# Seven block products of 256 columns in place of eight, for eleven channel pairs in two of four feed-forward passes

## The chip, the cores and the metric

The kernel runs on one core of a Trainium2 chip. The metric is the device time of one execution in microseconds. A core has TensorE (PE in the profile), VectorE (DVE), ScalarE (ACT), GpSimd (POOL) and SyncE (SP), which issues the DMAs. Each engine works through its own list of instructions in order and waits at semaphores for the others.

## What is computed

A trunk of two residual layers over 1024 tokens of width 1024, in float32. Layer 0 mixes tokens by gated and by sparse attention, layer 1 by a convolution module; each is followed by the same kind of feed-forward block, which is what the change touches:

```
def conv_ffn(x, w_up, conv_w, conv_b, w_down):
    h = causal_dwconv(x @ w_up, conv_w, conv_b)      # 1024 -> 5632 channels, 3 taps along the sequence
    g, u = jnp.split(h, 2, axis=-1)
    return (jax.nn.gelu(g) * u) @ w_down             # 2816 -> 1024
...
    for layer in range(DEPTH):
...
        x = layer_norm(ALPHA * x + mix, ln_mix_g[layer], ln_mix_b[layer])
        ffn = conv_ffn(x, ffn_w_up[layer], ffn_conv_w[layer], ffn_conv_b[layer], ffn_w_down[layer])
        x = layer_norm(ALPHA * x + ffn, ln_ffn_g[layer], ln_ffn_b[layer])
```

## The kernel before

The 1024 tokens are worked on in two halves of 512, so there are four feed-forward passes: `F00` (half 0, layer 0), `F10` (half 1, layer 0), `F01` (half 0, layer 1) and `F11` (half 1, layer 1). Every float32 product is made of three matmuls: each operand is split into a high part, rounded to the type fp32r, and a low remainder, and `mm3` (L76 to L79) adds high by low, low by high and high by high. `split` (L61) makes the high part on ACT and the low part by a subtraction on DVE or POOL; `wload` (L65) loads a block of weights of 128x1024 and splits it, the high part `wh` on ACT (L70), the low part `wl` in two halves on POOL (L73). There are three buffers each for the raw block `wraw`, for `wh` and for `wl`.

A pass has 22 channel pairs, a gate channel tile and a value channel tile of 128 channels each. `up(j)` computes the two tiles of pair j: eight blocks of the input width, 24 matmuls of 512 columns for each tile, into a PSUM bank `pu`. Then come the three convolution taps: ACT writes the first from PSUM to `acc` (L677), DVE adds the other two (L681, L682), and in half 0 the last two tokens are copied to `halo` (L684) for half 1, which computes its corrections `cor` from them at its start (L661 to L666). ACT takes the gelu of the gate tile (L687), POOL multiplies the two tiles (L689) and makes the low part `pl` of the product (L63), ACT its high part `ph`. The down product runs in three groups of 8, 8 and 6 pairs; a unit of it is 24 matmuls of 512 columns with one weight block, into the banks `pd`, which DVE adds to the residual `Z` (L396, L398). In the last pass the third group keeps its weights on chip and ends with the final layer norm, token tile by token tile (`down_last`).

A layer norm (`normed`, L623 and L624) works on `Z` with two vectors `gb`, of which there are two buffers; `norm` transposes the result on PE (`pn`, L635) and splits it into the next operand `XT`. The main program interleaves generators: each `yield` hands over to another chain. The order of the instructions on each engine is then set by a scheduler, within what the data and the buffers allow, so that it isn't the written one.

Of the kernel before, what the change touches and what calls it, by code (L numbers as in the profile page):

```python
# [10 lines left out]
F32 = mybir.dt.float32  # L11
F32R = mybir.dt.float32r
# [9 lines left out]
EPS = 1e-5  # L22
NPAIR = 22
KG = [(0, 8), (8, 16), (16, 22)]
FW = 1152
F2W = 256

# [10 lines left out]
def trunk_kernel(ctx, tc, xt, wab, wv, w280, wst, sgub, sgulg, sgulb, pe_k, pe_v, w1k, w1v, w2k, w2v,  # L38
# [10 lines left out]
    def A(tag, dtype=F32, shape=(128, 8, 512), name="A"):  # L49
        return ap.tile(list(shape), dtype, name=name, tag=tag, bufs=2)  # L50
# [25 lines left out]
    def mm3(out_, ah, al, bh, bl, first, last):  # L76
        nc.tensor.matmul(out_, ah, bl, start=first, stop=False)  # L77
        nc.tensor.matmul(out_, al, bh, start=False, stop=False)  # L78
        nc.tensor.matmul(out_, ah, bh, start=False, stop=last)  # L79

    def mtile(out_, w, xh, xl, kn=8):
        wh, wl = w
# [69 lines left out]
    def col(n, i):  # L152
        return V[n][:, i:i + 1]
# [448 lines left out]
    def tmp(name, w=512, bufs=4):  # L602
        return fp.tile([128, w], F32, name=name, tag="t", bufs=bufs)
# [47 lines left out]
    hal = fp.tile([128, 44, 2], F32, name="halo")  # L651
    cor = fp.tile([128, 44, 2], F32, name="cor")

    def ffn(h, l, tail=None):
        xh, xl = XT[h]
        z = Z[h]
        cw = V[f"fw{l}"].rearrange("p (m k) -> p m k", k=3)
# [8 lines left out]
                nc.vector.tensor_tensor(cor[:, :, i], cor[:, :, i], V[cb], op=OP.add)  # L666
        prod = {}

        def up(j):
            acc = []  # L670
            for e in range(2):
                mt = 2 * j + e
                w = wload(wup[l, mt])
                p = psn("u", "pu")
                mtile(p, w, xh, xl)
                a = tmp("acc")
                nc.scalar.activation(a[:, 2 * h:], p[:, 2 * h:], AF.Identity, scale=cw[:, mt, 2:3], bias=col(cb, mt))  # L677
                for i in range(2 * h):
                    nc.scalar.activation(a[:, i:i + 1], p[:, i:i + 1], AF.Identity, scale=cw[:, mt, 2:3],  # L679
                                         bias=cor[:, mt, i:i + 1])  # L680
                nc.vector.scalar_tensor_tensor(a[:, 1:], p[:, :511], cw[:, mt, 1:2], a[:, 1:], op0=OP.mult, op1=OP.add)  # L681
                nc.vector.scalar_tensor_tensor(a[:, 2:], p[:, :510], cw[:, mt, 0:1], a[:, 2:], op0=OP.mult, op1=OP.add)  # L682
                if h == 0:
                    nc.vector.tensor_copy(hal[:, mt, :], p[:, 510:512])  # L684
                acc.append(a)
                if e == 0:
                    nc.scalar.activation(a, a, AF.Gelu_apprx_tanh)  # L687
                    yield
            nc.gpsimd.tensor_tensor(acc[0], acc[0], acc[1], op=OP.mult)  # L689
            hi = fp.tile([128, 512], F32R, name="ph", tag="p", bufs=18)  # L690
            lo = fp.tile([128, 512], F32R, name="pl", tag="p", bufs=18)
            split(hi, lo, acc[0], nc.gpsimd)
            prod[j] = (hi, lo)
            yield

        def down_last(tail):
# [22 lines left out]
        def down(gi):  # L719
            j0, j1 = KG[gi]  # L720
            return product(lambda k: prod[j0 + k], lambda dh, b: wdn[l, gi * 8 + dh * 4 + b], j1 - j0,
                           into(h, gi == 0, gi == 2))

        done = 0
        for gi, (j0, j1) in enumerate(KG):
            top = min(j1 + 1, NPAIR)
# [255 lines left out]
```

## Time and profile before

| | |
|---|---|
| time, median of 3 runs | 2336.21 us (2334.55 to 2337.54) |
| the profiled execution | 2339.19 us |
| its span, first to last instruction | 2337.4 us |
| busy share of the span | PE 98%, DVE 50%, ACT 43%, POOL 59% |
| mean granted TensorE clock | 0.993 |

The first row is what the prediction is measured against. The durations of instructions come from one profiled execution, which is a little longer than the median. Its busy shares are means over stages that differ; what a stage is limited by is read from a stretch of it. Matmuls are pipelined: the time one of them takes in a row is longer than the distance between the starts of two of them, and it is the distance that counts.

### The profile page before, as it was taken

The page shows a single profiled execution, that of the slowest core. Times are in us where ns is not written, and L with a number is a line of the kernel's source. Part 1 is how long each engine was busy: PE and PEld are TensorE (multiplying, and loading weights), DVE is VectorE, ACT ScalarE, POOL GpSimd, SP SyncE. Part 2 cuts the span into 40 slices and gives each one's busy share as a digit, 9 for nine tenths or more (in the row PEclk, how much of TensorE's full clock was granted, in tenths as well). Part 3 has the DMA queues.
Part 4 walks back from the last instruction along what each step waited for, and adds up shares of the span by engine and source line. Part 5 has one row for each costly group of instructions (what it writes and reads, how often), then busy time and mean ns, then how long its engine had stood idle before and what let it go on. Part 6 is the DMA issues. An engine that isn't in the chain of part 4 may idle for free.

```text
span 2337.4 us, 30072 instructions
## 1 busy us (share of the span) xinstructions
PE 2295.2 (98%) x10959; PEld 1916.0 (82%) x10959; DVE 1174.3 (50%) x2144; ACT 1008.4 (43%) x1786; POOL 1390.4 (59%) x1313
## 2 busy tenths in 40 slices
PE   9999899999999999999999999999999999999998
PEld 7889789887888888788888887788888887888886
DVE  3532889656322223579972326589961446212214
ACT  4133998733433323433343552433242633534441
POOL 4442776566665656655566576655566666666672
PEclk9999999999999999999999999999999999999999
DMA  6053121353223323222323233232332233323340
GB/s 230 31 145 96 51 64 53 116 185 104 90 95 99 98 92 99 81 97 93 99 93 97 90 109 109 81 96 94 99 97 93 90 108 135 97 94 98 99 135 36
DMA packets 82987, 232.22 MB, mean 99 GB/s; under 512 B 10079, under 2 KB 24039, under 8 KB 82840
## 3 DMA queue, kind: packets, MB, share of 16 engines
q1 hardware_dynamic: 82840, 230.30, 31.0%
q8 instruction: 87, 1.43, 0.2%
q14 instruction: 60, 0.49, 0.1%
HBM read 213.44 MB, written 8.43 MB: 95 GB/s over the span
## 4 chain that ended last, share of the span: by engine, by line
PE 92%; DVE 3%; ACT 2%; issue 1%; POOL 1%; DMA 1%; DVEq 0%; ACTq 0%; SPq 0%; POOLq 0%
PE pu L77 14%; PE pu L79 13%; PE pu L78 13%; PE pd L77 9%; PE pd L78 9%; PE pd L79 9%; PE pt L562 2%; PE pcg L78 1%; PE pca L78 1%; PE pcg L77 1%; PE pca L77 1%; PE pca L79 1%; PE pcg L79 1%; DVE P L498 1%; PE O L570 1%
## 5 line engine op out<-in xcount | busy, mean ns | idle before, releaser
L73 POOL TENSOR_TENSOR wl<-wraw,wh 128x512 fp32r<-128x512 f32 x680 | 888.8, 1329 | 706.3 <-ACT wh L70 706.0
L77 PE MATMUL pu<-XTl,wh 128*128 128x512 f32 x1440 | 565.8, 393 | 5.5 <-DVE acc L682 3.7
L79 PE MATMUL pu<-XTh,wh 128*128 128x512 f32 x1440 | 564.2, 392 | 0.0
L78 PE MATMUL pu<-XTh,wl 128*128 128x512 f32 x1440 | 563.7, 391 | 0.0
L70 ACT ACTIVATE wh<-wraw 128x1024 fp32r<-128x1024 f32 x340 | 359.5, 1058 | 413.8 <-PE pd L79 349.1
L681 DVE SCALAR_TENSOR_TENSOR acc<-pu,vec,acc 128x511 f32<-128x511 f32 x176 | 131.7, 748 | 515.1 <-ACT acc L679 267.2
L77 PEld LDWEIGHTS pu<-XTl,wh 128*128 128x128 f32 x1440 | 272.5, 189 | 62.6 <-issue 4.1
L757 DVE SCALAR_TENSOR_TENSOR cacc<-ht,vec,cacc 128x512 f32<-128x512 f32 x464 | 318.5, 750 | 5.5 <-ACT cacc L753 3.9
L677 ACT ACTIVATE acc<-pu,vec 128x510 f32<-128x510 f32 (+1 forms) x176 | 137.1, 779 | 424.3 <-PE pu L79 424.1
L79 PEld LDWEIGHTS pu<-XTh,wh 128*128 128x128 f32 x1440 | 272.1, 189 | 56.7
L78 PEld LDWEIGHTS pu<-XTh,wl 128*128 128x128 f32 x1440 | 272.3, 189 | 56.3
L77 PE MATMUL pd<-wl,ph 128*128 128x512 f32 x656 | 259.2, 396 | 0.0
L78 PE MATMUL pd<-wh,pl 128*128 128x512 f32 x656 | 258.8, 395 | 0.0
L79 PE MATMUL pd<-wh,ph 128*128 128x512 f32 x656 | 256.8, 395 | 0.0
L79 PEld LDWEIGHTS pd<-wh,ph 128*128 128x128 f32 x656 | 123.6, 188 | 28.8
L78 PEld LDWEIGHTS pd<-wh,pl 128*128 128x128 f32 x656 | 123.7, 189 | 28.7
L77 PEld LDWEIGHTS pd<-wl,ph 128*128 128x128 f32 x656 | 123.6, 188 | 28.5
L398 DVE TENSOR_TENSOR Z<-Z,pd 128x512 f32<-128x512 f32 x64 | 43.5, 682 | 180.1 <-PE pd L79 180.0
L682 DVE SCALAR_TENSOR_TENSOR acc<-pu,vec,acc 128x510 f32<-128x510 f32 x176 | 131.5, 747 | 4.7
L689 POOL TENSOR_TENSOR acc<-acc 128x512 f32<-128x512 f32 x88 | 113.6, 1291 | 25.1 <-DVE acc L682 17.6
L396 DVE SCALAR_TENSOR_TENSOR Z<-Z,pd 128x512 f32<-128x512 f32 x64 | 43.6, 681 | 158.3 <-PE pd L79 158.3
L63 POOL TENSOR_TENSOR pl<-acc,ph 128x512 fp32r<-128x512 f32 x88 | 113.7, 1292 | 8.9 <-ACT ph L62 7.4
(251 smaller groups left out, 3778.1 us busy)
## 6 DMA issues: line engine op xcount, KB each, us to landing
wraw<-wup SPq DMA_DIRECT2D x176, 512.0 KB, 3.5
wraw<-wdn SPq DMA_DIRECT2D x82, 512.0 KB, 3.5
wraw<-cwin SPq DMA_DIRECT2D x32, 512.0 KB, 3.5
wraw<-wout SPq DMA_DIRECT2D x16, 512.0 KB, 4.0
wraw<-cwout SPq DMA_DIRECT2D x16, 512.0 KB, 3.5
wraw<-wab SPq DMA_DIRECT2D x14, 512.0 KB, 3.8
gb<-lns SPq DMA_DIRECT2D x12, 512.0 KB, 4.3
B<-fd SPq DMA_DIRECT2D x8, 512.0 KB, 3.8
```

The lines of the kernel that those rows point to most:

```text
L63: (leng or nc.vector).tensor_tensor(lo, src, hi.bitcast(F32), op=OP.subtract)
L70: nc.scalar.activation(wh[:, :n], raw[:, :n], AF.Copy)
L73: (leng or nc.gpsimd).tensor_tensor(wl[:, c], raw[:, c], wh[:, c].bitcast(F32), op=OP.subtract)
L77: nc.tensor.matmul(out_, ah, bl, start=first, stop=False)
L78: nc.tensor.matmul(out_, al, bh, start=False, stop=False)
L79: nc.tensor.matmul(out_, ah, bh, start=False, stop=last)
L562: nc.tensor.transpose(pt[:, j, e * 128:(e + 1) * 128], P[:, e, o:o + kn], ident)
L677: nc.scalar.activation(a[:, 2 * h:], p[:, 2 * h:], AF.Identity, scale=cw[:, mt, 2:3], bias=col(cb, mt))
L681: nc.vector.scalar_tensor_tensor(a[:, 1:], p[:, :511], cw[:, mt, 1:2], a[:, 1:], op0=OP.mult, op1=OP.add)
L682: nc.vector.scalar_tensor_tensor(a[:, 2:], p[:, :510], cw[:, mt, 0:1], a[:, 2:], op0=OP.mult, op1=OP.add)
L689: nc.gpsimd.tensor_tensor(acc[0], acc[0], acc[1], op=OP.mult)
L757: nc.vector.scalar_tensor_tensor(c[0] if k else ht[:, :H], ht[:, k:k + H], dww[:, j, k:k + 1], c[0], op0=OP.mult, op1=OP.add)
```

## The change

In `F00` and `F11` the pairs 5 to 15 are computed by `up7(j)`. It takes the two channel tiles of a pair, the two halves of the input width and the two halves of the 512 tokens as a 2 by 2 by 2 block product, and forms it from seven block products (Winograd's form of Strassen's method) where the plain form has eight. Each is four input blocks by three matmuls of 256 columns, so there are 84 such matmuls for a pair where there were 48 of 512 columns. The seven need sums of blocks of both operands. The sums of the weights are made per pair in `prep(j)`, by four additions on DVE (`ws` and in place in `wraw`), of which three results are split on ACT (`sh`) and DVE (`sl`); the raw blocks `ra` and `rb` themselves are split on ACT and POOL as before. The sums of the input (`TA`, `TB`) are made once per pass in `sums()`, on DVE, POOL and ACT, in the buffers that held the norm vectors, which are therefore loaded a second time for half 0's layer 0. The results are put together from the banks `pa` and `pb` and a copy `tt` by five additions of 256 columns on DVE. In all 22 pairs of these two passes the product of the two tiles and its split are on DVE instead of POOL (`gated`). The down product of these passes comes in units of 24 matmuls, one behind the fifth product of each pair, in groups of four pairs; each pass has 16 more additions to `Z` by that. The code that normalises half 1 is moved behind pair 15 of `F00`, that of the final norm of half 0 behind pair 5 of `F11`.

```diff
+QUICK = (5, 16)
...
-    def ffn(h, l, tail=None):
+    def ffn(h, l, tail=None, quick=False):
...
+        def gated(j, acc):
+            eng = nc.vector if quick else nc.gpsimd
+            eng.tensor_tensor(acc[0], acc[0], acc[1], op=OP.mult)
+            hi = fp.tile([128, 512], F32R, name="ph", tag="p", bufs=18)
+            lo = fp.tile([128, 512], F32R, name="pl", tag="p", bufs=18)
+            split(hi, lo, acc[0], eng)
...
+        def sums():
...
+            for k in (0, 2):
+                u1, u2 = (fp.tile([128, 2, 2, 256], F32, name="ts", tag="nrm", bufs=2) for _ in range(2))
+                b11, b12, b22, b21 = u1[:, 0], u1[:, 1], u2[:, 0], u2[:, 1]
+                nc.gpsimd.tensor_tensor(b11, *f(k, 0), op=OP.add)
+                nc.vector.tensor_tensor(b12, *f(k, 256), op=OP.add)
+                nc.gpsimd.tensor_tensor(b21, *f(k + 4, 0), op=OP.add)
+                nc.vector.tensor_tensor(b22, *f(k + 4, 256), op=OP.add)
+                nc.vector.tensor_tensor(b22, b22, b12, op=OP.subtract)
+                nc.vector.tensor_tensor(b12, b12, b11, op=OP.subtract)
+                nc.vector.tensor_tensor(b11, b22, b11, op=OP.add)
+                nc.vector.tensor_tensor(b21, b21, b11, op=OP.subtract)
+                yield
+                for n, t_, e in (("t2", b11, nc.vector), ("t1", b12, nc.vector), ("t3", b22, nc.gpsimd),
+                                 ("t4", b21, nc.vector)):
+                    split(X7[n][0][:, k:k + 2], X7[n][1][:, k:k + 2], t_, e)
+                yield
+
+        def prep(j):
+            ra, rb = W4(F32, name="wraw"), W4(F32, name="wraw")
+            nc.sync.dma_start(ra, wup[l, 2 * j])
+            nc.sync.dma_start(rb, wup[l, 2 * j + 1])
+            s1, s2 = (fp.tile([128, 512], F32, name="ws", tag="ht", bufs=8) for _ in range(2))
+            a, b = slice(0, 512), slice(512, 1024)
+            add = lambda o, x_, y_, op: nc.vector.tensor_tensor(o, x_, y_, op=op)
...
+            def pair(src):
+                h_, l_ = W4(F32R, name="wh", tag="wh"), W4(F32R, name="wl", tag="wl")
+                nc.scalar.activation(h_, src, AF.Copy)
+                for c in (a, b):
+                    nc.gpsimd.tensor_tensor(l_[:, c], src[:, c], h_[:, c].bitcast(F32), op=OP.subtract)
+                return [(h_[:, c], l_[:, c]) for c in (a, b)]
...
+            add(s1, rb[:, a], rb[:, b], OP.add)
+            add(s2, s1, ra[:, a], OP.subtract)
+            w["11"], w["12"] = pair(ra)
+            w["s2"] = one(s2, nc.vector)
+            w["s1"] = one(s1, nc.vector)
+            yield w
+            add(rb[:, a], ra[:, a], rb[:, a], OP.subtract)
+            add(ra[:, b], ra[:, b], s2, OP.subtract)
+            w["s3"], w["22"] = pair(rb)
+            w["s4"] = one(ra[:, b], nc.vector)
+            yield
...
+        def up7(j):
+            w = W7.pop(j)
+            pa, pb = psn("u", "pa"), psn("c", "pb")
+            t_ = tmp("tt")
+            t_, v_ = t_[:, :256], t_[:, 256:]
+            c0, c1 = slice(0, 256), slice(256, 512)
+            add = lambda o, a, b: nc.vector.tensor_tensor(o, a, b, op=OP.add)
+            prod7(pa[:, c0], w["11"], X7["11"])
+            prod7(pb[:, c1], w["s2"], X7["t2"])
+            nc.scalar.activation(t_, pa[:, c0], AF.Copy)
+            add(t_, t_, pb[:, c1])
+            prod7(pa[:, c0], w["12"], X7["21"], False)
+            nxt = prep(j + 1) if j + 1 < QUICK[1] else None
+            prod7(pa[:, c1], w["s1"], X7["t1"])
+            add(v_, t_, pa[:, c1])
+            if nxt:
+                W7[j + 1] = next(nxt)
+            prod7(pb[:, c0], w["s3"], X7["t3"])
+            add(pb[:, c1], v_, pb[:, c0])
+            yield
+            prod7(pa[:, c1], w["s4"], X7["22"], False)
+            add(pa[:, c1], t_, pa[:, c1])
+            acc = [taps3(2 * j, pa)]
+            nc.scalar.activation(acc[0], acc[0], AF.Gelu_apprx_tanh)
+            prod7(pb[:, c0], w["22"], X7["t4"], False)
+            if nxt:
+                next(nxt)
+            add(pb[:, c0], t_, pb[:, c0])
+            acc.append(taps3(2 * j + 1, pb))
+            gated(j, acc)
+            yield
...
-    F00 = ffn(0, 0)
-    mix(norm(1, g0), F00, 1)
-    go(F00, 56)
+    F00 = ffn(0, 0, quick=True)
+    go(F00, 2 * QUICK[1])
+    g0 = affine(0)
+    mix(norm(1, g0), F00, 2)
+    go(F00, 4)
...
+    F11 = ffn(1, 1, lambda tt: final(1, g3)(tt), quick=True)
+    go(F01)
+    go(F11, 2 * QUICK[0] + 2)
     g3 = affine(3)
-    F11 = ffn(1, 1, final(1, g3))
-    go(F01)
     for tt in range(4):
         final(0, g3)(tt)
-        go(F11, 2)
+        go(F11, 4)
     go(F11)
```

The order on PE in the middle of `F00` before, in the up product of a pair: one bank, three matmuls of 512 columns per input block.

```order
L79 MATMUL pu<-XTh,wh 128x512
L77 MATMUL pu<-XTl,wh 128x512
L78 MATMUL pu<-XTh,wl 128x512
L79 MATMUL pu<-XTh,wh 128x512
L77 MATMUL pu<-XTl,wh 128x512
L78 MATMUL pu<-XTh,wl 128x512
```

The order on PE in the same pass of the change, in the middle of a pair. `pa<-XTh,wl` and its like are the next pair's first product, `pb<-TB,wh` is the seventh product of the pair, on the columns of `pb` that the third of the sums (s3) was multiplied into.

```order
L81 MATMUL pa<-XTh,wh 128x256
L79 MATMUL pa<-XTl,wh 128x256
L80 MATMUL pa<-XTh,wl 128x256
L81 MATMUL pa<-XTh,wh 128x256
L79 MATMUL pb<-TB,wh 128x256
L80 MATMUL pb<-TB,wl 128x256
L81 MATMUL pb<-TB,wh 128x256
```

The products are half as wide, and products of two pairs stand between each other: the first product of the next pair runs ahead of the seventh of this one.

The order on DVE in `F00` before, for one pair: two taps and a halo copy for each tile.

```order
L681 SCALAR_TENSOR_TENSOR acc<-pu,vec,acc 128x511
L682 SCALAR_TENSOR_TENSOR acc<-pu,vec,acc 128x510
L684 COPY halo<-pu 128x2
L681 SCALAR_TENSOR_TENSOR acc<-pu,vec,acc 128x511
L682 SCALAR_TENSOR_TENSOR acc<-pu,vec,acc 128x510
L684 COPY halo<-pu 128x2
```

The order on DVE in `F00` of the change, the second half of a pair's period without `Z` additions: L64 is the low part of a sum of weights (`sl`) or of the product (`pl`), L685 the product, L724 a sum of weights, L771 an addition of 256 columns.

```order
L680 COPY halo<-pb 128x2
L64 TENSOR_TENSOR sl<-ws,sh 128x512
L685 TENSOR_TENSOR acc<-acc 128x512
L64 TENSOR_TENSOR pl<-acc,ph 128x512
L771 TENSOR_TENSOR tt<-tt,pa 128x256
L64 TENSOR_TENSOR sl<-ws,sh 128x512
L724 TENSOR_TENSOR wraw<-wraw,ws 128x512
L771 TENSOR_TENSOR pb<-tt,pb 128x256
L64 TENSOR_TENSOR sl<-wraw,sh 128x512
L771 TENSOR_TENSOR pa<-tt,pa 128x256
L677 SCALAR_TENSOR_TENSOR acc<-pa,vec,acc 128x511
L771 TENSOR_TENSOR pb<-tt,pb 128x256
```

The taps (now L677 and L678) have between them the weight work for the pair after next and the product and its split, which stood on POOL.

The order on POOL in `F00` before, over two pairs with no down unit between them.

```order
L73 TENSOR_TENSOR wl<-wraw,wh 128x512 x2
L689 TENSOR_TENSOR acc<-acc 128x512
L73 TENSOR_TENSOR wl<-wraw,wh 128x512 x2
L63 TENSOR_TENSOR pl<-acc,ph 128x512
L73 TENSOR_TENSOR wl<-wraw,wh 128x512 x2
L689 TENSOR_TENSOR acc<-acc 128x512
L73 TENSOR_TENSOR wl<-wraw,wh 128x512 x2
L63 TENSOR_TENSOR pl<-acc,ph 128x512
```

The order on POOL in `F00` of the change, from pair to pair: the four of L731 are two for `rb` and two for the next `ra`, L74 is the block of down weights.

```order
L731 TENSOR_TENSOR wl<-wraw,wh 128x512 x4
L74 TENSOR_TENSOR wl<-wraw,wh 128x512 x2
L731 TENSOR_TENSOR wl<-wraw,wh 128x512 x4
L74 TENSOR_TENSOR wl<-wraw,wh 128x512 x2
L731 TENSOR_TENSOR wl<-wraw,wh 128x512 x4
L74 TENSOR_TENSOR wl<-wraw,wh 128x512 x2
```

POOL keeps the splits of the unsummed weights alone, in a fixed order of ra, down, rb.

## Rows read from the trace of the kernel before

**Rows 1.** The head of the page: busy time by engine, the chain by engine.

```profile
PE 2295.2 (98%) x10959; PEld 1916.0 (82%) x10959; DVE 1174.3 (50%) x2144; ACT 1008.4 (43%) x1786; POOL 1390.4 (59%) x1313
...
PE 92%; DVE 3%; ACT 2%; issue 1%; POOL 1%; DMA 1%; DVEq 0%; ACTq 0%; SPq 0%; POOLq 0%
```

**Rows 2.** Busy time by window: up products and down products of half 0's pass.

```profile
core 0: us, PE busy (x) PEld busy (x) DVE busy (x) ACT busy (x) POOL busy (x), PEclk, DMA share, GB/s
604.90:659.30 54.40, 54.40 (x242) 45.05 (x241) 15.65 (x31) 23.02 (x31) 37.86 (x30) 1.00 0.31 97
668.90:713.40 44.50, 44.50 (x193) 36.09 (x192) 6.37 (x10) 9.66 (x10) 23.08 (x19) 1.00 0.31 97
```

**Rows 3.** Timeline of PE, 256 columns (start, duration), first and last of 11.

```profile
84.00 0.28 PE L78 MATMUL pg<-wsh,vl 128*128 128x256 f32 x1
...
85.18 0.28 PE L79 MATMUL pg<-wsh,vh 128*128 128x256 f32 x1
```

**Rows 4.** DVE: two neighbours on the timeline, and a group of 256 columns (mean).

```profile
492.39 0.69 DVE L63 TENSOR_TENSOR mt<-mraw,mt 128x512 fp32r<-128x512 f32 x1
493.00 0.69 DVE L400 BATCH_NORM_STATS2 st<-Z 128x6 f32<-128x512 f32 x1
...
L63 DVE TENSOR_TENSOR ptl<-pt,pth 128x256 fp32r<-128x256 f32 x24 | 9.9, 414 | 0.3
```

**Rows 5.** Timelines of ACT, DVE and POOL in one up product.

```profile
641.81 0.78 ACT L677 ACTIVATE acc<-pu,vec 128x512 f32<-128x512 f32 x1 [3.71 <-PE pu L79]
642.48 1.05 ACT L70 ACTIVATE wh<-wraw 128x1024 fp32r<-128x1024 f32 x1
643.43 0.62 ACT L62 ACTIVATE ph<-acc 128x512 fp32r<-128x512 f32 x1
...
643.47 0.75 DVE L682 SCALAR_TENSOR_TENSOR acc<-pu,vec,acc 128x510 f32<-128x510 f32 x1
644.14 0.15 DVE L684 COPY halo<-pu 128x2 f32<-128x2 f32 x1
...
643.61 2.54 POOL L73 TENSOR_TENSOR wl<-wraw,wh 128x512 fp32r<-128x512 f32 x2 [1.65 <-ACT wh L70]
```

**Rows 6.** DMA issues: size of each, microseconds from issue to landing.

```profile
wraw<-wup SPq DMA_DIRECT2D x176, 512.0 KB, 3.5
```

**Rows 7.** Timeline of DVE, correction step of `F10`, POOL quiet.

```profile
905.33 0.19 DVE L663 TENSOR_TENSOR cor<-cor,cor 128x44 f32<-128x44 f32 x1
```

**Rows 8.** Timelines of DVE and POOL, the same step in `F11`.

```profile
1884.83 1.33 DVE L664 TENSOR_TENSOR cor<-halo,vec 128x44 f32<-128x44 f32 x1
1886.08 1.32 DVE L663 TENSOR_TENSOR cor<-cor,cor 128x44 f32<-128x44 f32 x1
...
1884.79 1.30 POOL L63 TENSOR_TENSOR Sl<-nrm,Sh 128x512 fp32r<-128x512 f32 x1
1886.05 1.29 POOL L689 TENSOR_TENSOR acc<-acc 128x512 f32<-128x512 f32 x1
```

**Rows 9.** Timelines of DVE and POOL, final norm at half 1's last pass.

```profile
1959.14 1.28 DVE L623 SCALAR_TENSOR_TENSOR Z<-Z,mv,gb 128x1024 f32<-128x1024 f32 x1
...
1970.06 2.11 DVE L623 SCALAR_TENSOR_TENSOR Z<-Z,mv,gb 128x1024 f32<-128x1024 f32 x1
...
1969.80 3.49 POOL L73 TENSOR_TENSOR wl<-wraw,wh 128x512 fp32r<-128x512 f32 x2
```

**Rows 10.** Timeline of PE at the starts of `F00` and `F11`.

```profile
577.25 1.71 PE L635 MATMUL pn<-ident,Z 128*128 128x128 f32 x8 [2.73 <-DVE XTl L63]
578.66 0.77 PE L77 MATMUL pu<-XTl,wh 128*128 128x512 f32 x1
...
585.41 0.82 PE L635 MATMUL pn<-ident,Z 128*128 128x128 f32 x6
...
1975.18 0.77 PE L77 MATMUL pu<-XTl,wh 128*128 128x512 f32 x1 [3.75 <-DVE acc L682]
```

**Rows 11.** Busy time by window, behind the first stall (eighth value: granted clock).

```profile
578.70:581.00 2.30, 2.30 (x8) 1.82 (x7) 2.30 (x2) 1.97 (x3) 0.78 (x1) 0.50 0.36 148
```

More of the change, by code (lines that the diff above doesn't have):

```diff
@@ L74, in wload, with mm3 @@
         return wh, wl
[L76 to L79, printed above, removed]
+    def mm3(out_, ah, al, bh, bl, first, last, more=False):
+        nc.tensor.matmul(out_, ah, bl, start=first, stop=False, skip_group_check=more)
+        nc.tensor.matmul(out_, al, bh, start=False, stop=False, skip_group_check=more)
+        nc.tensor.matmul(out_, ah, bh, start=False, stop=last, skip_group_check=more)
     def mtile(out_, w, xh, xl, kn=8):
@@ L667, in ffn, with taps3 @@
         prod = {}
+        def taps3(mt, p):
+            a = tmp("acc")
+            nc.scalar.activation(a[:, 2 * h:], p[:, 2 * h:], AF.Identity, scale=cw[:, mt, 2:3], bias=col(cb, mt))
+            for i in range(2 * h):
+                nc.scalar.activation(a[:, i:i + 1], p[:, i:i + 1], AF.Identity, scale=cw[:, mt, 2:3],
+                                     bias=cor[:, mt, i:i + 1])
+            nc.vector.scalar_tensor_tensor(a[:, 1:], p[:, :511], cw[:, mt, 1:2], a[:, 1:], op0=OP.mult, op1=OP.add)
+            nc.vector.scalar_tensor_tensor(a[:, 2:], p[:, :510], cw[:, mt, 0:1], a[:, 2:], op0=OP.mult, op1=OP.add)
+            if h == 0:
+                nc.vector.tensor_copy(hal[:, mt, :], p[:, 510:512])
+            return a
@@ new lines, in prep, with one @@
+        def prep(j):
[5 more added lines that the diff above has]
+            add = lambda o, x_, y_, op: nc.vector.tensor_tensor(o, x_, y_, op=op)
+            w = {}
+            def pair(src):
[4 more added lines that the diff above has]
+                return [(h_[:, c], l_[:, c]) for c in (a, b)]
+            def one(src, eng):
+                h_, l_ = (fp.tile([128, 512], F32R, name=n, tag="ht", bufs=8) for n in ("sh", "sl"))
+                split(h_, l_, src, eng)
+                return h_, l_
+            add(s1, rb[:, a], rb[:, b], OP.add)
[9 more added lines that the diff above has]
+            yield
@@ new lines, in prod7, with lead7 @@
+        def prod7(o, w, x_, first=True):
+            for k in range(4):
+                s_ = slice(k * 128, (k + 1) * 128)
+                mm3(o, w[0][:, s_], w[1][:, s_], x_[0][:, k, :], x_[1][:, k, :], first and k == 0, k == 3, not first)
+        W7 = {}
+        def lead7():
+            if QUICK[0] not in W7:
+                W7[-1] = prep(QUICK[0])
+                W7[QUICK[0]] = next(W7[-1])
+            else:
+                next(W7.pop(-1), None)
+        def up7(j):
[29 more added lines that the diff above has]
+            yield
@@ L675, in up @@
                 mtile(p, w, xh, xl)
[L676 to L685, printed above, removed]
+                acc.append(taps3(mt, p))
                 if e == 0:
-                    nc.scalar.activation(a, a, AF.Gelu_apprx_tanh)
+                    nc.scalar.activation(acc[0], acc[0], AF.Gelu_apprx_tanh)
                     yield
[L689 to L693, printed above, removed]
+            gated(j, acc)
             yield
@@ L722, in down, with downs @@
                            into(h, gi == 0, gi == 2))
+        if quick:
+            src = lambda a, dh, i: wdn[l, (a + 2 * i) // 8 * 8 + dh * 4 + (a // 2 + i) % 4]
+            def downs():
+                units = [(a, dh, i) for a in range(0, 16, 4) for dh in range(2) for i in range(2)]
+                w = wload(src(*units[0]))
+                yield
+                for n, (a, dh, i) in enumerate(units):
+                    if i == 0:
+                        p = [psn("d", "pd") for _ in range(4)]
+                        done = into(h, a == 0, False)
+                    for tt in range(4):
+                        ts = slice(tt * 128, (tt + 1) * 128)
+                        for k in range(2):
+                            (ah, al), s_ = prod[a + 2 * i + k], slice(k * 512, k * 512 + 512)
+                            mm3(p[tt], ah[:, ts], al[:, ts], w[0][:, s_], w[1][:, s_], i == k == 0, i == k == 1)
+                        if i:
+                            done(tt, dh, p[tt])
+                    if n + 1 < len(units):
+                        w = wload(src(*units[n + 1]))
+                    yield
+            dn, sm = downs(), sums()
+            last = down_last(tail) if tail else None
+            for j in range(NPAIR):
+                for i, _ in enumerate(up7(j) if QUICK[0] <= j < QUICK[1] else up(j)):
+                    if i == (j < 4) and j >= 3:
+                        next(dn, None)
+                    if (i if j in (1, 2) else j in (3, 4)) and next(sm, 1):
+                        lead7()
+                    if tail and 16 <= j < 19:
+                        next(last)
+                    yield
+            yield from last if tail else product(lambda k: prod[16 + k], lambda dh, i: src(16, dh, i), 6,
+                                                 into(h, False, True))
+            return
         done = 0
```

7 lines of the change are left out of this document (added).

## The prediction

> **What bounds the kernel now.** I read the head of the page first. TensorE is busy 98% of the span and carries 92% of the chain that ended last [rows 1]; the profiled execution took 2339.19 us, 1.8 us more than its span and 3.0 us more than the median of the runs. Then I cut one stretch of each kind out of half 0's first feed-forward pass [rows 2]. In the stretch of up products PE is busy all 54.40 us, ten products of 24 matmuls, so 5.44 us a product and 226.7 ns a matmul. In the stretch of down products PE is again busy throughout: 192 matmuls in 44.50 us, 5.56 us per unit of 24. In the up stretch VectorE (DVE) works 15.65 us, 3.1 us per pair, and GpSimd (POOL) 37.86 us, 7.6 per pair. So PE sets the pace, and DVE has over two thirds of its time free. A pair and one down unit take 2x5.44 + 5.56 = **16.44 us**. The change touches 22 such pairs, 362 us, and gives DVE and POOL new work exactly there.
>
> **PE's share.** Out go 48 matmuls of 512 columns per pair, in come 84 of 256. The products named pg are the nearest row: 256 columns, a fresh weight load before each, 11 starts from 84.00 to 85.18, so 118 ns [rows 3]. Half of a 512-column matmul is 113.4 ns. So a pair costs 84x0.118 = 9.91 us (9.53 by the other bound) in place of 10.88. I take 0.118, a row of the same width. With the unit PE alone would need **15.47 us**, 0.97 less than now (1.35 by the bound): over 22 pairs -21.4 us (-29.7). The Trainium skill gives another price ("TensorE: Matmul & The Clock Gate", Back-to-back issue gap): 262 cycles for 256 columns, 109 ns at 2.4 GHz, by which the pair would take 9.2 us and the 22 pairs 37 us less than now. The same table's 518 cycles for 512 columns are 216 ns, and the trace has 226.7, so the measurement decides.
>
> **DVE's new work.** Start-to-start distances price it: two 512-column operations on SBUF alone stand 0.61 us apart [rows 4]; a tap and its successor 0.67 us [rows 5]; a 256-column operation lasts 0.414 us [rows 4], and since the 512-column ones last 0.69 and start every 0.61, I put it at 0.34. Per pair DVE gets nine operations with both inputs in SBUF (four L724, three sl, the product L685 and its split pl): 5.5 us; four taps, 2.7; two halo copies, 0.1; five additions of 256 columns, 1.7. That is 10.0 us. Every second pair also has four Z additions, 2.4 us. Mean 11.2 of 15.47: DVE alone would not be the bound.
> POOL keeps six splits per pair, two each for ra, for the down weights and for rb: 2.54 us each two [rows 5], so 7.5 us. ACT has three 1024-column conversions at 0.95 (642.48 to 643.43), two first taps at 0.67, five operations near 0.55 and a short copy [rows 5]: 7.2 us. Neither is the bound alone. Bytes are as before, and each load lands in 3.5 us [rows 6].
>
> **What the sum leaves out.** In the correction step, five additions and products of only 44 columns on DVE. With POOL quiet one takes 0.19 us [rows 7]. With POOL working back to back, each takes 1.32 to 1.33 us and starts 1.25 us after the last, as far apart as POOL's own operations [rows 8]. They take turns: a DVE operation with both inputs in SBUF stands behind a whole POOL operation, then POOL stands behind it. The layer norm's 1024-column step shows the same at another size: 1.28 us, or 2.11 beside POOL [rows 9]. The taps, which read PSUM, do not stretch: 0.75 us at 643.47, with POOL at work from 643.61 [rows 5]. The Trainium skill says so too ("SBUF — State Buffer", Who interferes with whom): the two engines share one port pair, held for a whole instruction, and a DVE instruction with two SBUF inputs contends with a GpSimd one that reads SBUF. By that rule the change is at its weakest here, since DVE now has nine such operations per pair and before had none in the up products.
> So DVE needs between 10.0 us (12.4 with Z), if no POOL operation meets it, and 11.2+6x1.25 = 18.7 us on average, if all six do. Which holds depends on the order.
>
> **The walk round one pair.** Product seven adds onto the columns of pb that product three left, so it waits for DVE's addition pb<-tt,pb (fifth row of the PE order and eighth of the DVE order in the section on the change). I put time 0 at the end of that addition. PE: product seven ends at 1.5, 7 matmuls of product two and the unit at 7.9, products three to five at 12.1, and 29 more matmuls bring it to the next product seven at 15.5.
> DVE and POOL, two-input operations taking turns: the split sl of s4 and the addition to pa end at 1.0; ACT's first tap at 1.8, DVE's taps and the pb addition at 3.6. ACT converts rb into the buffer that product seven frees, 1.8 to 2.8, so POOL splits rb from 2.9 to 5.4. DVE's first weight sum is ready at 3.6, but its raw block has been loading into the slot that the s4 split freed (about 3.5 us and SP's issue, 4.3 at the earliest); POOL takes the second split from 4.15, and the sum runs 5.4 to 6.0. Then a tap, two sums, a 256 addition, a tap and a halo copy to 9.0, and sl to 9.6. Meanwhile the unit has ended, ACT has converted ra (8.0 to 9.1) and POOL's two splits of ra are due. From here they alternate: POOL to 10.8, the product to 11.4, POOL to 12.7, pl to 13.3, the addition for product six to 13.6 (PE asks for it at 13.5, so about 0.2 lost), POOL's first down split to 14.5, sl to 15.1, POOL to 16.4, the last weight sum to 17.0 and the awaited addition to **17.3**. PE stood ready at 15.5: a wait of about 1.8 us, where PE waits on nothing now. With the four Z additions, which partly fill DVE's waits, I get 18.3. Half of each: 17.8 for half 0's pass; half 1's has no halo copies and one-column steps on ACT instead, and I put it at 17.6. The mean, 17.7, is 1.26 over 16.44: 22x1.26 = **+28 us**.
>
> **The rest.** The operand sums add, per pass, 18 DVE operations (11 us) and six POOL ones (7.5 us), in the first pairs, where DVE is free two thirds of the time. They take turns there with POOL and with the layer norm steps, whose DVE part the scheduler puts straight behind them in both passes, though the program moves final(0) and norm(1) later. The stalls there now are 2.73 us before transposes in half 0's pass and 3.75 before a product in half 1's [rows 10]; neither cause is gone. I take +3 us, the size of one more such stall, with bounds 0 and +7.5 (both again). Two reloaded norm vectors hide under DMA; uncovered they would cost 3.5 us each. The 16 more Z additions per pass are in the DVE sum. Down matmuls, their order by units of 24 included, keep their number and length.
> Sum on the profiled execution: 2339.2 + 28 + 3 = 2370; on the median of the runs, 3.0 lower: **2367**.
>
> **Rivals.**
> *PE stays the bound (faster).* If the addition is ready by 15.5, the port's turns are hidden and the pair takes 15.5: 2336 - 21 + 3 = 2318, or 2310 at 113.4 ns. The point that decides: the walk must shorten by 1.8 us, one and a half of the four POOL operations that stand between 9.6 and 16.4. For it speaks that DVE has 4 us free over the pair, and that the down splits would only have to come two operations later or earlier; against it, that POOL's order puts ra, down, rb one after another and none can start before ACT's conversion.
> *Half of it.* If one POOL operation less meets DVE in that stretch, the mean is 17.7 - 1.25 = 16.4 and the time 2336 + 0 + 3, about 2338: no change within 0.2% (4.7 us, about what a measurement can tell here).
> *The clock gives way too.* After the stall at 577 PE took 6.75 us for the 24 matmuls from 578.66 to 585.41, against 5.44 [rows 10]; the granted clock from 578.7 to 581.0 was 0.50, the lower of the two levels (1.2 of 2.4 GHz) [rows 11]. Stalls of 1.8 us every pair could cost up to 1.3 us each more: 2367 + 29 = 2396. Against it: PE is still busy nine tenths of each pair, and the stall of each would be two thirds as long as that one.
> *Every POOL operation meets DVE:* 18.7 per pair, +50 and +3: 2389.
>
> **Chances and range.** The walk (16.7 to 18.3 per pair, so 2345 to 2380) 0.50; PE-bound, or close to it, 0.31; half 0.11; clock or full alternation 0.08. The first and last are slower, so faster 0.31, same 0.11, slower 0.58. Of the PE-bound cases I leave the better part of the low bound out, and of the dear ones the clock case: 2315 to 2388 leaves about 0.2 outside.
>
> **What would show it.** Right: in the pairs from the sixth on, 256-column matmuls 118 ns apart, with a gap of 1 to 3 us before product seven on pb, released by DVE's addition; L724, L685 and L64 on DVE averaging 1.0 us or more instead of 0.69; POOL's splits well over 1.3 [rows 8]; pairs 17 to 18 us apart; no new gap elsewhere but at the passes' starts. Wrong: DVE's two-input operations near 0.7 us, or stretched with no gap on PE, and pairs 15.5 apart, which would make it PE-bound; a gap before product three or a unit would mean that a weight load or split is late instead, which my walk has in time; 256-column spacings well over 118 ns would make PE's own share a loss.

## The result, and the profile after

The changed kernel took 2365.8 us in the median (2362.6 to 2370.6), 1.0125 times the kernel before (interval 1.0103 to 1.0146): 1.25% slower, where 2367 was forecast. The profiled execution took 2366.99 us. Of the page's head, the rows that answer to [rows 1]:

```profile
span 2365.3 us, 32215 instructions
PE 2286.7 (97%) x11751; PEld 1940.0 (82%) x11751; DVE 1495.8 (63%) x2564; ACT 1061.5 (45%) x1890; POOL 1337.4 (57%) x1237
...
PE 76%; DVE 12%; issue 4%; DMA 3%; ACT 3%; POOL 1%; SPq 0%; DVEq 0%; ACTq 0%; POOLq 0%
```

PE's share of the chain that ended last fell from 92% to 76%; DVE, issue, the loads and ACT took the difference. The windows run from the first matmul of one down unit to that of another nine pairs later, in the first pass and in the last (the eighth value is the granted clock):

```profile
656.23:812.99 156.76, 144.89 (x975) 131.14 (x974) 130.22 (x197) 68.65 (x101) 81.00 (x56) 1.00 0.27 92
2067.15:2223.58 156.43, 144.68 (x974) 132.24 (x973) 132.72 (x180) 78.57 (x137) 82.65 (x55) 0.99 0.29 95
```

A pair with its unit took 156.76/9 = 17.42 us and 17.38, against 16.44 before [rows 2], and DVE was busy 14.5 us of it. PE stood idle 12 us of each stretch, at a mean granted clock of 1.00 and 0.99. What it waited for, in the table of waits of the whole execution (total us, times, longest):

```profile
PE pb L79 <- DVE pb L771: 16.3, 15, 1.4
PE pu L79 <- DVE acc L678: 8.1, 2, 6.2
PE pu L79 <- DVE halo L680: 6.2, 2, 3.9
...
PE pa L79 <- DVE tt L771: 3.9, 8, 0.8
```

The first is the wait before product seven, the last the one before product six, each where the walk put it. (The columns of pb that product seven adds onto are those that product five, with the third sum s3, has written; the prediction calls it product three, and no term hangs on that.) The rows of 3.9 and 6.2 us are stalls at the starts of the passes. The chain that ended last, in one pair with Z additions (start, duration):

```profile
777.19 4.50 DMA wraw<-wup
...
783.99 0.60 DVE ws L724
784.59 0.60 DVE wraw L724
...
787.12 1.09 DVE sl L64
788.20 1.69 DVE acc L685
...
791.51 1.78 DVE sl L64
793.28 0.61 DVE wraw L724
793.98 0.64 ACT sh L63
794.64 0.69 DVE sl L64
795.34 0.35 DVE pa L771
```

It runs from the load of a raw block through DVE to the end of the pair. Timelines of DVE, POOL and PE in the next pair, without Z additions, on the same stretch:

```profile
798.62 0.74 DVE L724 TENSOR_TENSOR ws<-wraw 128x512 f32<-128x512 f32 x1 [0.29 <-DMA wraw<-wup]
...
802.64 0.67 DVE L64 TENSOR_TENSOR sl<-ws,sh 128x512 fp32r<-128x512 f32 x1
803.24 1.78 DVE L685 TENSOR_TENSOR acc<-acc 128x512 f32<-128x512 f32 x1
...
807.19 1.37 DVE L64 TENSOR_TENSOR sl<-ws,sh 128x512 fp32r<-128x512 f32 x1
808.48 1.77 DVE L724 TENSOR_TENSOR wraw<-wraw,ws 128x512 f32<-128x512 f32 x1
810.17 0.42 DVE L771 TENSOR_TENSOR pb<-tt,pb 128x256 f32<-128x256 f32 x1
...
803.01 3.17 POOL L731 TENSOR_TENSOR wl<-wraw,wh 128x512 fp32r<-128x512 f32 x2 [2.50 <-ACT wh L729]
806.72 2.99 POOL L74 TENSOR_TENSOR wl<-wraw,wh 128x512 fp32r<-128x512 f32 x2 [0.54 <-ACT wh L71]
...
810.64 0.39 PE L79 MATMUL pb<-TB,wh 128*128 128x256 f32 x1 [1.25 <-DVE pb L771]
```

With POOL's splits of ra from 803.0 and of the down block from 806.7, DVE's product, split and weight sum last 1.78, 1.37 and 1.77 us instead of 0.69, POOL's two take 3.0 to 3.2 instead of 2.54 [rows 5], and PE waits 1.25 us. Over nine pairs of the first pass, by groups (mean ns; idle before, releaser):

```profile
L64 DVE TENSOR_TENSOR sl<-ws,sh 128x512 fp32r<-128x512 f32 x18 | 21.9, 1217 | 0.4
...
L685 DVE TENSOR_TENSOR acc<-acc 128x512 f32<-128x512 f32 x9 | 12.7, 1410 | 0.0
L724 DVE TENSOR_TENSOR wraw<-wraw,ws 128x512 f32<-128x512 f32 x9 | 12.0, 1333 | 0.0
...
L64 DVE TENSOR_TENSOR pl<-acc,ph 128x512 fp32r<-128x512 f32 x9 | 10.0, 1115 | 2.9 <-ACT ph L63 2.9
...
L724 DVE TENSOR_TENSOR ws<-wraw 128x512 f32<-128x512 f32 x9 | 7.4, 819 | 11.1 <-DMA wraw<-wup 11.0
```

The first four, five operations per pair, last 2.8 us more per pair than at 0.69 each; all nine two-input operations average 1.03 us and last 3.1 us more per pair. The last row is the other part of the chain: DVE stood idle 11.0 us, 1.2 per pair, for the load of rb. In the nine pairs of the last pass it is 4.7 us, 0.5 per pair, and the nine operations last 3.4 us more there.

The passes' starts answer to [rows 10]. PE's waits there, and DVE just ahead of the longest:

```profile
579.03 0.77 PE L79 MATMUL pu<-XTl,wh 128*128 128x512 f32 x1 [3.93 <-DVE halo L680]
...
2008.54 0.77 PE L79 MATMUL pu<-XTl,wh 128*128 128x512 f32 x1 [6.19 <-DVE acc L678]
...
1998.88 4.65 DVE L625 SCALAR_TENSOR_TENSOR Z<-Z,mv,gb 128x1024 f32<-128x1024 f32 x2 [1.41 <-DMA gb<-lns]
```

I count as lost what the distances between PE's matmul starts add up to over the median of their shape and bank. By that PE lost 13.8 us before the first pass's steady pairs and 13.4 before the last's, where the kernel before lost 4.8 and 6.6 at these starts; 17.0 and 16.7 in the nine pairs of each pass, where it lost none; and next to nothing in the two other seven-product pairs of each pass. The stall of 2.7 us before the transposes of the next norm step, at 958 us before, is still there, at 976 us.

### The profile page after: what moved, and what is told of

It reads as the page before. It is cut to its first block, busy times and chain, and to the rows that moved or that the text cites. A ratio compares the mean times of both kernels' runs of the same rounds, so it can differ in the third digit from the quotient of the medians.

```text
span 2365.3 us, 32215 instructions
## 1 busy us (share of the span) xinstructions
PE 2286.7 (97%) x11751; PEld 1940.0 (82%) x11751; DVE 1495.8 (63%) x2564; ACT 1061.5 (45%) x1890; POOL 1337.4 (57%) x1237
## 4 chain that ended last, share of the span: by engine, by line
PE 76%; DVE 12%; issue 4%; DMA 3%; ACT 3%; POOL 1%; SPq 0%; DVEq 0%; ACTq 0%; POOLq 0%
PE pu L79 10%; PE pu L80 9%; PE pu L81 9%; PE pd L79 8%; PE pd L80 8%; PE pd L81 8%; DMA wraw<-wup 2%; PE pt L564 2%; DVE wraw L724 2%; DVE sl L64 1%; PE pcg L79 1%; PE pca L79 1%; PE pcg L81 1%; PE pca L81 1%; PE pca L80 1%
## 5 line engine op out<-in xcount | busy, mean ns | idle before, releaser
L74 POOL TENSOR_TENSOR wl<-wraw,wh 128x512 fp32r<-128x512 f32 x592 | 803.7, 1381 | 603.6 <-ACT wh L71 591.8
L79 PE MATMUL pu<-XTl,wh 128*128 128x512 f32 x1088 | 430.2, 395 | 19.0 <-DVE acc L678 8.1
L80 PE MATMUL pu<-XTh,wl 128*128 128x512 f32 x1088 | 428.1, 393 | 0.0
L81 PE MATMUL pu<-XTh,wh 128*128 128x512 f32 x1088 | 428.0, 393 | 0.0
L677 DVE SCALAR_TENSOR_TENSOR acc<-pu,vec,acc 128x511 f32<-128x511 f32 x132 | 98.6, 747 | 266.9 <-ACT acc L675 136.9
L79 PEld LDWEIGHTS pu<-XTl,wh 128*128 128x128 f32 x1088 | 206.8, 190 | 64.7 <-ACT TB L63 7.9
L81 PEld LDWEIGHTS pu<-XTh,wh 128*128 128x128 f32 x1088 | 206.7, 190 | 43.4
L80 PEld LDWEIGHTS pu<-XTh,wl 128*128 128x128 f32 x1088 | 206.7, 190 | 42.5
L673 ACT ACTIVATE acc<-pu,vec 128x512 f32<-128x512 f32 (+1 forms) x132 | 102.9, 780 | 280.0 <-PE pu L81 279.9
L731 POOL TENSOR_TENSOR wl<-wraw,wh 128x512 fp32r<-128x512 f32 x88 | 126.8, 1463 | 175.5 <-ACT wh L729 175.5
L64 DVE TENSOR_TENSOR ptl<-pt,pth 128x512 fp32r<-128x512 f32 (+1 forms) x160 | 101.0, 645 | 29.9 <-ACT pth L63 22.0
L541 POOL TENSOR_SCALAR P<-P,sm 128x64 f32<-128x64 f32 (+6 forms) x192 | 107.2, 583 | 16.2 <-DVE sm L535 7.8
L508 ACT ACTIVATE P<-P,mx 128x64 f32<-128x64 f32 (+6 forms) x192 | 115.1, 613 | 2.2 <-DVE mx L500 2.1
```

Source lines behind the costliest of these rows:

```text
L79: nc.tensor.matmul(out_, ah, bl, start=first, stop=False, skip_group_check=more)
L80: nc.tensor.matmul(out_, al, bh, start=False, stop=False, skip_group_check=more)
L81: nc.tensor.matmul(out_, ah, bh, start=False, stop=last, skip_group_check=more)
L508: nc.scalar.activation(P[:, e, o:o + ln_], P[:, e, o:o + ln_], AF.Exp, bias=mx[:, e, mi:mi + 1], scale=-1.0, accum_out=sm[:, e, i:i + 1])
L541: nc.gpsimd.tensor_scalar(P[:, e, o:o + ln_], P[:, e, o:o + ln_], sm[:, e, i:i + 1], 0.0, op0=OP.mult, op1=OP.add)
L731: nc.gpsimd.tensor_tensor(l_[:, c], src[:, c], h_[:, c].bitcast(F32), op=OP.subtract)
```

## The experiments

Two theories stood after the result. Theory 1: turns at the port between DVE's and POOL's operations on SBUF, in the stretch before the awaited addition, make it late. Rival 2: the three raw buffers do, since rb cannot load before the s4 split has freed its slot.

**POOL's work taken away.** All of it but the down block's:

```diff
-                for c in (a, b):
-                    nc.gpsimd.tensor_tensor(l_[:, c], src[:, c], h_[:, c].bitcast(F32), op=OP.subtract)
-                return [(h_[:, c], l_[:, c]) for c in (a, b)]
+                return [(h_[:, c], h_[:, c]) for c in (a, b)]
```

> The changed kernel, but the seven-product pairs leave out the low part of the raw weights ra and rb (the high part is used in its place), so POOL has only the two splits of the down block per pair. PE does the same matmuls. Theory 1 (DVE's two-input operations and POOL's take turns at a shared port, and the two splits of ra and two of the down block stand between DVE's last operations and the addition that product seven waits for): pairs of 15.5 to 15.9 us instead of 17.4, L64, L685 and L724 near 0.7 us, 22 x 1.6 = 35 us less, 2326 to 2336 us. Rival 2 (the wait of DVE's first weight sum for the load of rb, 2 us in a pair looked at, carries the loss, since only three raw buffers rotate): that wait is still there, pairs of 17 us or more, 2358 to 2366 us.

2337.5 us (ratio to the kernel before 1.0006, 0.9997 to 1.0015), pairs of 141.00/9 = 15.67 us in the first pass. The wait for the load had not gone; it was longer. The table of waits over these nine pairs, and two of DVE's groups:

```profile
DVE ws L724 <- DMA wraw<-wup: 13.9, 9, 3.3
...
PEld pb L79 <- DVE pb L769: 0.2, 1, 0.2
...
L724 DVE TENSOR_TENSOR wraw<-wraw,ws 128x512 f32<-128x512 f32 x9 | 8.9, 987 | 0.0
...
L685 DVE TENSOR_TENSOR acc<-acc 128x512 f32<-128x512 f32 x9 | 7.1, 789 | 0.0
```

The turns are not all gone, since the down block's splits remain: the nine operations average 0.84 us and last 1.4 us more per pair, in place of 3.1. The load's wait does not carry the loss by itself: with it in place and the turns more than halved, PE lost 1.7 us in these nine pairs in place of 17.0. The time is 1.5 us above the range that I gave; the starts are unchanged (13.8 us lost in each).

**The same amount taken away at two places.** As above, but with the return only for `src is ra`, or only for `src is rb`.

> The changed kernel, in which the low part of the raw weights ra alone is left out (the high part is used in its place); rb keeps its two splits on POOL. Two of POOL's six operations per pair are gone, those that stand in the walk between 9.6 and 12.7 us, ahead of the addition that product seven waits for. Theory 1 (turns at the port in that stretch): 2.5 us off 17.4, so PE-bound but for the pairs with Z additions: 15.5 to 16.0 us a pair, 2330 to 2338 us. Rival (POOL's share of the port as a whole matters, wherever it falls): the same as without the splits of rb.

> The changed kernel, in which the low part of the raw weights rb alone is left out; ra keeps its splits. As many POOL operations are gone as without those of ra, but they stand in the walk between 2.9 and 5.4 us, where DVE waits for the load of its next raw block anyway. DVE's order is that of the changed kernel. Theory 1: at most 0.5 us a pair, 16.9 to 17.4 us, 2355 to 2366 us. Rival (POOL's share of the port as a whole): 15.5 to 16.0 us a pair, 2330 to 2338 us, as without those of ra.

Without ra's splits 2344.7 us, pairs of 16.0 and 16.4; without rb's 2357.7 us, pairs of 16.76 and 16.73 (windows of nine, eight, seven and seven pairs). The waits before product seven in the whole execution, without ra's and without rb's:

```profile
PE pb L79 <- DVE pb L774: 4.3, 4, 1.3
```

```profile
PE pb L79 <- DVE pb L774: 14.3, 13, 2.3
```

As much POOL work is worth 1.2 us a pair where the walk meets it and 0.7 where DVE mostly waits for the load or works on taps (in the changed kernel's first pass rb's two splits took 2.55 us in seven of the nine pairs, as long as with DVE quiet), so the place counts, as theory 1 has it. It was too simple by half: ra's came out 7 us dearer than I wrote, rb's at 0.7 rather than at most 0.5, and without ra's the scheduler changed DVE's order too, which it did not without rb's. Nor is rb's 0.7 the same in all pairs: in the seven pairs of the first pass those without Z additions took 15.5 us and those with them 18.0 to 18.8, as long as with the splits or longer.

**More raw buffers.**

```diff
-            ra, rb = W4(F32, name="wraw"), W4(F32, name="wraw")
+            ra, rb = fp.tile([128, 1024], F32, name="wraw", tag="nrm", bufs=2), W4(F32, name="wraw")
...
-    go(F11, 2 * QUICK[0] + 2)
+    go(F11, 2 * QUICK[1])
     g3 = affine(3)
...
-        go(F11, 4)
+        go(F11, 2)
```

> The changed kernel, with the raw block ra in the two buffers of the norm vectors, so that five raw buffers serve the pairs; the norm vectors of half 1 in the first pass, and of half 0 in the last, can then only be loaded when the last pair of seven products has let go of them, and the norm steps stand in the plain pairs behind. The weight sums stand ahead of the taps on DVE now. Theory 1: POOL's work is as before and takes turns with DVE's, but three two-input operations have moved out of the stretch before the awaited addition; DVE's two-input operations still average 0.9 us or more, pairs 15.6 to 16.4 us, time 2366 - 22 x 1.4 = 2335 us, and some 8 less for the norm steps that no longer stand in the passes' starts: 2320 to 2338 us. Rival 2: no wait for a load any more, pairs 15.5 us, time 2316 to 2330 us. A time of 2355 or more would speak against both.

2331.8 us, ratio 0.9979 (0.9970 to 0.9989): 0.2% faster than the kernel before. The windows, eight pairs in the first pass and in the last:

```profile
647.60:771.00 123.40, 123.40 (x866) 115.02 (x865) 111.65 (x179) 60.24 (x89) 74.96 (x48) 1.00 0.31 103
2037.90:2167.80 129.90, 125.10 (x867) 115.52 (x866) 118.11 (x164) 67.74 (x121) 73.20 (x49) 1.00 0.29 98
```

In the first pass PE never stops: 123.40/8 = **15.43 us** a pair, the 15.47 of the prediction's sum for PE. The turns are still there. Groups over these eight pairs:

```profile
L64 DVE TENSOR_TENSOR sl<-ws,sh 128x512 fp32r<-128x512 f32 x16 | 18.0, 1123 | 1.0 <-ACT sh L63 0.2
L724 DVE TENSOR_TENSOR wraw<-wraw,ws 128x512 f32<-128x512 f32 x8 | 14.2, 1777 | 0.0
...
L724 DVE TENSOR_TENSOR ws<-wraw 128x512 f32<-128x512 f32 x9 | 6.1, 679 | 0.0
```

The weight sum takes its 1.78 us in every pair, and PE does not see it, since DVE begins the weight work ahead of the taps and is never idle for a load. So neither theory is the whole cause: the load's wait and the turns lie one behind the other in DVE's chain, and PE waits for what of their sum is over its slack. In the first pass's steady pairs that sum (the nine operations' time over 0.69 us each, and the wait) is 4.3 us a pair in the changed kernel, 3.7 without rb's splits, 3.4 without ra's, 2.9 without both and 2.4 with five buffers; PE lost 1.9, 1.2, 0.5, 0.2 and 0.0 us a pair. The load's share alone is not isolated by that, since the five buffers change DVE's order too. In the last pass every second pair still took 16.8 us. The norm steps moved out of the starts as well: PE lost 5.9 and 4.8 us there, about as before the change, but 4.4 and 6.3 us behind the steady pairs, where the norm steps stand now.

**The product and its split back on POOL.** `eng = nc.gpsimd` in `gated`.

> The changed kernel, with the product of the two tiles and its split back on POOL in both passes. DVE has seven two-input operations per pair instead of nine, POOL eight instead of six. Theory 1: as many turns as before meet in the stretch, DVE shorter by 1.2 us and POOL longer by 2.5 us: pairs 16.8 to 18 us, time 2355 to 2378 us. Rival 2: the load's wait is unchanged and DVE's chain is 1.2 us shorter: pairs 16.2 us, time 2338 to 2345 us.

2369.5 us (1.0145, 1.0130 to 1.0160), pairs of 158.20/9 = 17.6 and 17.3: DVE's chain is 1.2 us shorter and nothing is won, so rival 2's time is excluded and theory 1's holds. Its reason holds in part only: DVE's seven operations last 2.2 us more per pair than at 0.69 each, where the nine lasted 3.1 more, but its wait for the load rose from 1.2 to 2.3 us a pair.

**The starts.** `sums` without its operations, the products taking blocks of `XT` for the sums.

> The changed kernel without the sums of the input blocks: the products take blocks of the input itself in their place (as many matmuls), so 18 DVE and 6 POOL operations per pass are left out in its first pairs. PE lost 13.8 us in the first 96 us of the first pass and 13.4 in the first 112 of the last, where the kernel before lost 4.8 and 6.6 in such stretches. If the sums cause that: 6 to 7 us lost in each, the pairs unchanged, time 2366 - 14 = 2349 to 2355 us. Rival: the norm steps of 1024 columns, loaded and run behind the sums, cause it: they then run earlier and the time is within 5 us of 2366.

2350.2 us (1.0055). PE lost 5.7 and 8.1 us in the starts, 13.4 less in all, and 16.8 and 15.5 in the steady pairs, nearly as much as with the sums. The time is the one that I wrote for the sums as the cause, and the rival is excluded. But the version with five buffers has the sums and its norm steps elsewhere, and it lost only 10.7 us in both starts. So it is sums and norm steps on top of each other that fill DVE; that fits both runs, and neither shows it alone, since the five buffers change DVE's order too.

**Operations moved to the other side of the port**, from the five-buffer version. One weight sum on POOL, then also the product and its split in the plain pairs:

```diff
-            add(ra[:, b], ra[:, b], s2, OP.subtract)
+            nc.gpsimd.tensor_tensor(ra[:, b], ra[:, b], s2, op=OP.subtract)
```

```diff
-            eng = nc.vector if quick else nc.gpsimd
+            eng = nc.vector if quick and QUICK[0] <= j < QUICK[1] else nc.gpsimd
```

> The version with five raw buffers, with the last sum of weights (ra's second half minus s2) on POOL instead of DVE. DVE has eight two-input operations per pair and POOL seven. In the last pass of the five-buffer version every second pair, the one with Z additions, took 16.8 us because that sum took 1.77 us in front of the awaited addition. Theory 1: those pairs fall to 15.5 to 16.0, 4 to 6 us off 2332: 2325 to 2329 us. Rival: POOL's additional operation takes the port as long elsewhere in the pair and the time is within 3 us of 2332.

> As the version with the sum on POOL, and the product and its split of the eleven plain pairs of each pass back on POOL, as in the kernel before. In the plain pairs the norm steps and the sums of the input blocks have two DVE operations per pair less to stand behind; POOL has two more. Theory 1: PE loses less at the passes' starts and behind the last pair of seven products, where 5.9, 5.0, 9.5 and 6.3 us were lost: 5 to 10 us less than the version with the sum on POOL, 2316 to 2323 us. Rival: POOL's turns become longer queues for the norm steps, no gain or up to 5 us worse, 2326 to 2333 us.

2342.3 and 2348.7 us: 10 us more than with five buffers, and 6 more again. Both expectations failed, and so did their rivals. The pairs with Z additions of the last pass fell to 16.1, but those of the first rose to 16.6 or 16.7, and new stalls came in behind the steady pairs: PE waited 4.0 us in the first pass and 7.2 us in the last for ACT's short copy tt.

**The down weights' low part on DVE**, from the changed kernel and from the five-buffer version; then one of rb's two splits as well (`e_ = nc.vector if src is rb and c is b else nc.gpsimd`); then the down weights in the last pass alone (`leng=nc.vector if tail else None`).

```diff
-                w = wload(src(*units[0]))
+                w = wload(src(*units[0]), leng=nc.vector)
...
-                        w = wload(src(*units[n + 1]))
+                        w = wload(src(*units[n + 1]), leng=nc.vector)
```

> The changed kernel, with the low part of the down weights of both passes' 16 units made on DVE instead of POOL. A two-input operation holds the port 0.6 us on DVE and 1.25 on POOL, so the port has 1.3 us less to do per pair, but DVE 1.2 us more (11 two-input operations, POOL four). Theory 1: two of the four POOL operations in the stretch ahead of the awaited addition are gone, 2.5 us less there and 1.2 more: pairs of 16.0 to 16.7 us, 2340 to 2352 us. Rival (DVE's own length sets the pair): 18 us or more, 2375 us.

> The version with five raw buffers, with the low part of the down weights of both passes' units on DVE. Theory 1: all pairs but those with Z additions stay at 15.4; in the last pass those with Z additions fall from 16.8 to 15.5 to 16.3: 2 to 6 us off 2332, 2326 to 2330 us. Rival (as with the weight sum on POOL, where one operation moved and the pairs with Z additions of the first pass rose to 16.7: what counts is where the scheduler then puts the others): 2332 to 2345 us.

> As the version before, with one of the two splits of rb on DVE as well: DVE has twelve two-input operations per pair, 13.0 us of work, 14.2 in pairs with Z additions mean 14.2, and POOL three. Theory 1: near or over PE's 15.4 us in the pairs with Z additions, where DVE alone needs 15.4: 16 us there, 2328 to 2336 us. Rival (the port's total is what counts, and it is 0.65 us smaller again): 2322 to 2328 us.

> The version with five raw buffers, with the low part of the down weights on DVE in the last pass alone; the order on DVE is that of the five-buffer version up to the last pass and that of the version with the splits on DVE in it. Theory 1 (where product seven is not reached by POOL's turns, the pass is PE-bound): the first pass as in the five-buffer version, in the last 3.6 us less lost than there (7.9 against 11.5 from 2040 to 2200 us): 2326 to 2331 us, faster than the kernel before by 0.25 to 0.45%. Rival: the difference between those two lies within what repeats of one kernel differ by, 2331 to 2335 us.

From the changed kernel 2372.9 us, not the 2340 to 2352 that I wrote. The rival's 2375 is near, but not for its reason: DVE was busy 148 us of 180 in the first pass and 153 of 190 in the last. POOL's operations were fewer, but the waits of PE moved. The first row is of the whole execution, the others are timelines round one of these waits:

```profile
PE pa L79 <- ACT tt L774: 23.3, 7, 4.1
...
757.64 0.69 DVE L724 TENSOR_TENSOR ws<-wraw 128x512 f32<-128x512 f32 x1 [1.55 <-DMA wraw<-wup]
758.37 1.66 DVE L724 TENSOR_TENSOR ws<-ws,wraw 128x512 f32<-128x512 f32 x1
759.95 1.75 DVE L724 TENSOR_TENSOR wraw<-wraw 128x512 f32<-128x512 f32 x1
761.62 0.41 DVE L771 TENSOR_TENSOR pb<-tt,pb 128x256 f32<-128x256 f32 x1
...
757.85 3.30 POOL L731 TENSOR_TENSOR wl<-wraw,wh 128x512 fp32r<-128x512 f32 x2 [9.89 <-ACT wh L729]
...
762.75 0.37 ACT L774 ACTIVATE tt<-pa 128x256 f32<-128x256 f32 x1
...
763.17 0.39 PE L79 MATMUL pa<-XTl,wh 128*128 128x256 f32 x1 [3.99 <-ACT tt L774]
```

The order of DVE and ACT had changed: the copy tt, which product three of `pa` waits for, stood on ACT behind the first tap of pb, and that behind DVE's addition to pb, which now had the load's wait and the weight sums in front of it, two of them at 1.66 and 1.75 us beside POOL's splits of rb. So the same two delays came out at another place, and PE lost up to 4 us at a time.

From the five-buffer version 2334.4 us (0.9991, 0.9983 to 1.0000; the rival held) and, with one of rb's splits too, 2334.5 (0.9995; as expected): no gain, and the wait for tt took 11.5 and 13.7 us there. With the last pass alone 2329.9 us, 0.9964 (0.9950 to 0.9977), the fastest of all, but its interval overlaps that of the five-buffer version, so that it beats the kernel before is shown, and that it beats the other isn't. Its trace speaks against it: the last pass's pairs took 15.5 us, as expected, but PE lost more behind them, and from 2040 to 2200 us it lost 11.4 us, as with five buffers (11.5), not the 7.9 that I had reckoned with.

## Why the prediction was right

**PE's share** held: 15.43 us a pair where nothing else limits, against 15.47; the seven products are worth 1.0 us a pair on PE.

**The wait before product seven** held in place, releaser and cause, and in the steady pairs its size came out a little smaller: 17.4 us a pair against 17.7. In the walk, pairs without Z additions were put at 17.3 and those with at 18.3; the two pairs shown took 16.95 and 18.05. What the walk had as one cause with a detail, the runs showed as two in a row: the load that DVE's first weight sum waits for took 4.5 us in the pair shown, not 3.5, and DVE's wait for it adds to the turns.

**The pairs' term** was mis-sized all the same, because it lets all 22 pairs pay. Eighteen did; in the other four PE lost nothing. From the first matmul of the first seven-product pair to the end of the eleventh the two passes took 195.5 and 195.6 us. The kernel before, at the distances of [rows 2], needs 188.2 and 189.1 us for the same pairs and the down and plain products that stand among them. So the pairs cost 7.3 + 6.5 = 14 us, half of the 28.

**The rest** was mis-sized the other way: +3 us, with bounds of 0 and 7.5, and 29 - 14 = 15 measured. I priced the sums and the norm steps as one more stall of the old size; in the two starts PE lost 27.2 us where it had lost 11.4, 16 us more. The miss of 14 us in the pairs and of 12 here cancelled. That the total came within 2 us is luck; what the prediction had right is the mechanism in the pairs and the direction.

**The rivals.** PE-bound: not in this kernel, but 1.8 us was a fair distance, for with five buffers the first pass was. The clock: 1.00 through the first pass's steady pairs, with waits of up to 1.25 us, so not in the way the rival had it; one longer wait in the last pass was followed by the lower level, as the last section shows. All six of POOL's operations meeting DVE: 18.7 was not reached; most of rb's fall beside DVE's wait for the load and its taps, which the runs without ra's and without rb's splits tell apart.

## What to carry to other kernels

Before a matmul saving is paid for with elementwise work, follow one period on the engine that gets the work, from the load that it starts with to the matmul that waits for it, and count what shares a port with it by its place and not by its sum. Where two delays lie one behind the other ahead of a slack, it is enough to bring their sum under it, by either of them; the cheap way here was two buffers that lay idle in these pairs, at the price of norm steps that had to move. Moving single operations between engines under a scheduler changes the orders of all of them, and of the seven such tries here one beat what it started from, and that one not clearly.

## What had not been expected of the hardware

In the first pass's nine steady pairs PE stood idle 12 us in all, in waits of up to 1.25 us, and its granted clock stayed at 1.00. In the last pass's nine there was one wait of 2.64 us, for DVE's low part of a weight sum, and the clock behind it (eighth value) fell to the lower of its two levels, as after the stall of 2.73 us in the kernel before [rows 11]; from 2086 us on it was 1.00 again, with waits of up to 1.42 us. A row of PE's timeline and a window:

```profile
2079.99 0.38 PE L80 MATMUL pb<-TA,sl 128*128 128x256 f32 x1 [2.64 <-DVE sl L64]
...
2082.00:2084.00 2.00, 2.00 (x11) 2.00 (x11) 1.58 (x4) 0.63 (x1) 0.00 (x0) 0.50 0.80 258
```

And a load's time to land was no constant. The page's median for the up weights is 3.3 us, but it lies over two lines of the program: ra's loads took 3.3 to 3.5 us, those of rb, which DVE's first weight sum waits for, 3.1 to 5.0 with a median of 4.1. So a place in the order that is right by the page's median can still be a wait.
